# Attention scores of two heads as three products on half-height tiles, in place of two full-height products for each head

## Chip, cores and metric

The kernel runs on one core of a Trainium2 chip. The metric is device time in microseconds (us) of one execution. Engines are named as the profile names them: PE is TensorE's matmul, PEld its weight load, DVE is VectorE, ACT is ScalarE, POOL is GpSimd, SP is SyncE, which issues most DMAs.

## What is computed

One decoder layer on 512 tokens of width 1024, in float32: an RMSNorm, one input projection, two branches (an mLSTM with 4 heads of 128 and an attention with 8 heads of 64), gates, and an output projection added to the input. The change is in the attention scores. Blocks are 256 tokens long and the top 3 past blocks are taken, of which 512 tokens have at most one, so the attention is causal over all tokens. Cut to what matters:

```python
q = _rmsnorm(at_q.reshape(ha), q_norm_w)          # ha = (1, 512, 8, 64)
k = _rmsnorm(at_k.reshape(ha), k_norm_w)
...
s_own = jnp.einsum('bhqd,bhsd->bhqs', q_c, k_own) * scale - slopes[:, None, None] * dist_own
s_own = jnp.where(dist_own >= 0, s_own, -jnp.inf)
...
p = jax.nn.softmax(s_all, axis=-1)
```

`slopes` of head h is 2^-(h+1).

## The kernel before

[...] To keep float32 accuracy each operand is split into an upper part (the value cast to `float32r`, on ACT) and a lower part (the rest, a subtraction on DVE), and a product is a sum of upper x upper, upper x lower and lower x upper. The projections are done so, three products of 512 columns for each 128 rows of the contraction; they make up most of PE's work.

The attention works by pairs of heads, `g_pair(p)` for p = 0 to 3. PE transposes the pair's 128 columns of q and of k into a PSUM bank, 64 rows for either head. `g_q` and `g_k` then make three buffers for each head u: `qs[u]`, whose 64 own rows hold the upper part of q and whose other 64 rows hold the lower part; `kh[u]`, with the upper part of k in both halves; `kl[u]`, with the lower part of k in both halves. All these instructions work on 64 rows of 512 columns. With q's two parts stacked, a product over 128 rows with `kh` gives two of the terms at once, and one with `kl` the others. `g_attn(h, ...)` runs for one head: a POOL instruction scales the distances by the slope (`eh`), and for each of four row tiles `g_tile(i)` issues two products of 256, 256, 384 and 512 columns into one bank. DVE adds distances and finds the row's minimum, ACT exponentiates, DVE and POOL divide by the sum; `g_pt` transposes the result, and the second head's generator runs the products with v for both heads, as tiles of 128 rows by 64 columns, one for either head.

Nothing is issued when these functions call the engines. `Schedule` records each instruction with its estimated cost (`cost`, lines 219 to 248) and its dependencies, and `issue` sorts all engines' instructions by list scheduling; the order in which PE, DVE, ACT, POOL and SP then run is fixed. Any cost that changes can move instructions anywhere in the program. Nearly all instructions carry one line of the helper that issues them, L256.

Of the kernel before, what the change touches and what calls it, by code (L numbers as in the profile page):

```python
# [17 lines left out]
P = 128  # L18
# [171 lines left out]
class Schedule:  # L190
# [28 lines left out]
    def cost(self, eng, name, out, ins, args, kw):  # L219
        n = 1  # L220
        for d in (args[1] if name == "tensor_reduce" else out).shape[1:]:
            n *= d
        if name.startswith("dma"):
            return 1000.0 if eng == "gpsimd" else 100.0
        if eng == "tensor":
            if name == "transpose":
                return 109.0
            n = 1
            for d in kw["rhs"].shape[1:]:
                n *= d  # L230
            if kw["rhs"].dtype == F32R:
                return max(0.452 * n, 60.0) + 2.0
            return max(n, 64) * 4 * (0.43 if out.shape[0] == P else 0.21)
        if eng == "scalar":
            c = 180.0 + 0.85 * n
            if name == "activation":
                c += 95.0 * sum(isinstance(kw.get(k), bass.AP) for k in ("scale", "bias"))
            return c + (190.0 if "accum_out" in kw else 0.0)
        if eng == "gpsimd":
            return 330.0 + 190.0 * n if kw.get("op") == ALU.pow else 380.0 + 1.05 * n  # L240
        if name == "tensor_tensor_scan":
            return 1210.0
        if name == "tensor_copy" and not any(r[0].startswith("bank") for r in ins):
            return 160.0 + 0.52 * n
        c = 155.0 + 1.04 * n
        if name == "scalar_tensor_tensor" and len(ins) > 2:
            c += 60.0
        return c + (83.0 if "accum_out" in kw else 0.0)

    def add(self, eng, name, fn, args, kw):  # L250
# [125 lines left out]
def hybrid_layer(ctx: ExitStack, tc: tile.TileContext, xT, x, w_in, w_out, smalls, out):  # L376
# [40 lines left out]
    def transpose(out_, in_, idn):  # L417
        plan.now += 107.0
        nc.tensor.transpose(out_, in_, idn)
# [3 lines left out]
    def tiny(n):  # L423
        ntiny[0] += n
        return tinies[:, ntiny[0] - n:ntiny[0]]
# [152 lines left out]
    def need_w(name, kk):  # L578
        plan.until(lambda: (name, kk) in W)
        return W[name, kk]  # L580


    ident = sb("ident", [P, P])
    make_identity(tc.nc, ident)
# [222 lines left out]
    offs = [0, 128, 384, 768]  # L807

    def g_pair(p):
        rank = 5 + p / 100  # L810
        yield when(lambda: have["q"] == NT and have["k"] == NT and br.ok(6) and (p < 2 or 2 * p - 3 in pts))
        qs, kh, kl = ([br.get() for _ in range(2)] for _ in range(3))
        qw, kw = sm[:, C_QW:C_QW + 1], sm[:, C_KW:C_KW + 1]
        mine, other = (slice(0, 64), slice(64, 128)), (slice(64, 128), slice(0, 64))
        done = []

        def turn(src):
            ps = banks.get()
            for t in range(NT):
                transpose(ps[:, t * P:(t + 1) * P], src[:, t, p * P:(p + 1) * P], ident)  # L820
            have["A"] += 1
            return ps

        def g_q():
            yield pe_bank()
            ps = turn(tq)
            yield plan.now + SLACK
            for u in range(2):
                r = mine[u]
                t_ = act.activation(qs[u][r], ps[r], AF.Copy, scale=qw[r])  # L830
            yield t_
            for u in range(2):
                r = mine[u]
                t_ = dve.scalar_tensor_tensor(qs[u][other[u]], ps[r], qw[r], qs[u][r].bitcast(F32),
                                              op0=ALU.mult, op1=ALU.subtract)
            banks.put(t_, ps)
            done.append(t_)

        def g_k():
            yield pe_bank()  # L840
            ps = turn(tk)
            yield plan.now + SLACK
            for u in range(2):
                r = mine[u]
                t_ = act.activation(kh[u][r], ps[r], AF.Copy, scale=kw[r])
            yield t_
            for u in range(2):
                r = mine[u]
                act.activation(kh[u][other[u]], ps[r], AF.Copy, scale=kw[r])
                dve.scalar_tensor_tensor(kl[u][r], ps[r], kw[r], kh[u][r].bitcast(F32),  # L850
                                         op0=ALU.mult, op1=ALU.subtract)
                t_ = dve.tensor_copy(kl[u][other[u]], kl[u][r].bitcast(F32))
            t_ = max(t_, act.clock + SLACK)
            banks.put(t_, ps)
            done.append(t_)

        plan.add(g_q(), rank)
        plan.add(g_k(), rank)
        yield when(lambda: len(done) == 2)
        for u in range(2):  # L860
            plan.add(g_attn(2 * p + u, qs[u], kh[u], kl[u], max(done)), rank + u / 200)

    def g_attn(h, qs, kh, kl, t0):
        rank = 5 + h / 200
        yield when(lambda: b2.ok() and b5.ok() and (h < 2 or h - 2 in pts))
        eh, pr = b2.get(), b5.get()
        te = pool.tensor_scalar(eh, dist, 2.0 ** -(h + 1), 0.0, op0=ALU.mult, op1=ALU.add)
        mn, sums, rec = (tiny(NT) for _ in range(3))
        done = {"p": 0, "t": 0}
        at = [t0]  # L870

        def finish(key, t):
            at[0] = max(at[0], t)
            done[key] += 1

        def g_tile(i):
            n = P * (i + 1)
            nn = max(n, 256)
            yield pe_bank(max(at[0], te))
            ps = banks.get()  # L880
            ts = slice(i * P, (i + 1) * P)
            mm(ps[:, :nn], qs[:, ts], kh[:, :nn], True, False)
            mm(ps[:, :nn], qs[:, ts], kl[:, :nn], False, True)
            yield plan.now + SLACK
            p_ = pr[:, offs[i]:offs[i] + n]
            t_ = dve.tensor_tensor_reduce(p_, ps[:, :n], eh[:, S - n:], scale=-1.0, scalar=BIG,
                                          op0=ALU.add, op1=ALU.min, accum_out=mn[:, i:i + 1])
            banks.put(t_, ps)
            yield t_
            yield act.activation(p_, p_, AF.Exp, scale=-1.0, bias=mn[:, i:i + 1], accum_out=sums[:, i:i + 1])  # L890
            have["exp"] += 1
            dve.reciprocal(rec[:, i:i + 1], sums[:, i:i + 1])
            yield dve.clock + SLACK
            finish("p", pool.tensor_scalar(p_, p_, rec[:, i:i + 1], 1.0, op0=ALU.mult, op1=ALU.mult))

        def g_pt(a, blocks, pt):
            yield pe_bank(at[0])
            ps = banks.get()
            n = P * len(blocks)
            for b, (i, j) in enumerate(blocks):  # L900
                transpose(ps[:, b * P:(b + 1) * P], pr[:, offs[i] + j * P:offs[i] + (j + 1) * P], ident)
            yield plan.now + SLACK
            t_ = (act.copy, dve.tensor_copy, act.copy)[a](pt[:, 512 * a:512 * a + n], ps[:, :n])
            banks.put(t_, ps)
            finish("t", t_)

        for i in range(NT):
            plan.add(g_tile(i), rank)
        yield when(lambda: done["p"] == NT and b5.ok())
        b2.put(plan.now, eh)  # L910
        br.put(plan.now, qs, kh, kl)
        pt = b5.get()
        for a, blocks in enumerate(([(0, 0), (1, 0), (2, 0), (3, 0)],
                                    [(1, 1), (2, 1), (3, 1), (3, 3)],
                                    [(2, 2), (3, 2)])):
            plan.add(g_pt(a, blocks, pt), rank)
        yield when(lambda: done["t"] == 3)
        b5.put(plan.now, pr)
        pts[h] = (pt, [pt[:, 0:512], pt[:, 512:896], pt[:, 1024:1280], pt[:, 896:1024]], at[0])
        if h % 2 == 0:  # L920
            return
        yield when(lambda: h - 1 in pts and have["v"] == NT)
# [12 lines left out]
        have["at"] += 1  # L935
# [694 lines left out]
```

## Time and profile before

| | |
|---|---|
| median of 3 runs | 303.6 us (303.38 to 303.67) |
| profiled execution | 303.79 us |
| its span, first to last instruction | 302.1 us |
| granted TensorE clock, mean | 0.998 |
| busy, share of the span: PE, PEld, DVE, ACT, POOL | 98, 79, 75, 61, 27% |

The span leaves out 1.7 us around the instructions. [...] In the timeline, consecutive instructions with the same names are merged into a row with a count and the first one's shape. A `float32` product that is not a transpose leaves two records.

### The profile page before, as it was taken

The numbers are of one execution on the slowest core, as the hardware profiler recorded it, in microseconds if no ns is written. First come the engines' busy times: TensorE is split into PE (matmuls) and PEld (weight loads), VectorE is DVE, ScalarE is ACT, GpSimd is POOL, SyncE is SP. The second block draws the span as 40 slices with busy tenths as digits, with TensorE's granted clock in tenths as the row PEclk, the third lists the DMA queues.
The fourth block names the chain that finished last, engine by engine and source line by source line (L and its number), as shares of the span: only waits on it lengthen the run. The fifth ranks groups of instructions, "written<-read, shape, count | busy, mean of one in ns | idle before, by whom it ended". The sixth has DMA issues, their size and how long they took to land.

```text
span 302.1 us, 4336 instructions
## 1 busy us (share of the span) xinstructions
PE 296.0 (98%) x1534; PEld 239.5 (79%) x1534; DVE 226.0 (75%) x473; ACT 184.0 (61%) x327; POOL 82.5 (27%) x93
## 2 busy tenths in 40 slices
PE   8999999999999999999999999999999999999995
PEld 3999888888888888688678868578889987787784
DVE  4896979698788868968669988620348858799992
ACT  3594648874639718543767946993963526688500
POOL 3000201059440370127127017541001146131200
PEclk9999999999999999999999999999999999999999
DMA  6994793552224112203004040926007699964344
GB/s 202 397 415 189 190 285 104 106 172 94 84 72 150 60 69 72 69 0 106 37 1 141 0 139 2 301 47 138 3 1 219 158 288 245 203 142 69 47 148 154
DMA packets 13381, 40.19 MB, mean 133 GB/s; under 512 B 1584, under 2 KB 1840, under 8 KB 13360
## 3 DMA queue, kind: packets, MB, share of 16 engines
q1 hardware_dynamic: 10640, 32.05, 30.2%
q0 software_dynamic: 2720, 7.87, 15.2%
q8 instruction: 12, 0.20, 0.3%
q14 instruction: 9, 0.07, 0.1%
HBM read 37.81 MB, written 2.10 MB: 132 GB/s over the span
## 4 chain that ended last, share of the span: by engine, by line
PE 96%; DMA 1%; ACT 1%; DVE 1%; issue 1%; SPq 0%
PE bank L256 96%; DMA b<-in_w_in_dram 1%; DVE b L256 0%; ACT whi L256 0%; ACT br L256 0%; ACT xh L256 0%; DVE whi L256 0%; SPq L256 0%; SPq L369 0%
## 5 line engine op out<-in xcount | busy, mean ns | idle before, releaser
L256 PE MATMUL bank<-whi,xh 128*128 128x512 f32 (+2 forms) x220 | 70.8, 365 | 0.4 <-DVE whi L256 0.2
L256 PE MATMUL bank<-whi,xl 128*128 128x512 f32 (+2 forms) x220 | 70.5, 360 | 0.0
L256 PE MATMUL bank<-wlo,xh 128*128 128x512 f32 (+2 forms) x220 | 70.3, 359 | 0.0
L256 DVE TENSOR_TENSOR wlo<-raw,whi 128x1024 fp32r<-128x1024 f32 x35 | 43.6, 1248 | 3.2 <-ACT whi L256 2.9
L256 ACT CAST whi<-raw 128x1024 fp32r<-128x1024 f32 x35 | 36.7, 1047 | 14.2 <-PE bank L256 14.0
L256 PEld LDWEIGHTS bank<-whi,xh 128*128 128x128 f32 x220 | 38.5, 192 | 8.2 <-ACT xh L256 1.1
L256 PEld LDWEIGHTS bank<-whi,xl 128*128 128x128 f32 x220 | 37.9, 188 | 6.3 <-issue 0.2
L256 PEld LDWEIGHTS bank<-wlo,xh 128*128 128x128 f32 x220 | 37.9, 188 | 6.1
L256 POOL TENSOR_SCALAR b<-b,tinies 128x128 f32<-128x128 f32 (+3 forms) x32 | 31.8, 1007 | 39.0 <-DVE tinies L256 38.4
L256 PE MATMUL bank<-xh,whi 128*128 128x512 f32 x96 | 39.3, 410 | 0.0
L256 PE MATMUL bank<-xh,wlo 128*128 128x512 f32 x96 | 38.3, 400 | 0.0
L256 PE MATMUL bank<-xl,whi 128*128 128x512 f32 x96 | 38.1, 398 | 0.0
L256 PE MATMUL bank<-whi,br 128*128 128x512 f32 x112 | 36.1, 397 | 0.8 <-ACT br L256 0.8
L256 PEld LDWEIGHTS bank<-whi,br 128*128 128x128 f32 x112 | 21.0, 188 | 6.0 <-ACT br L256 1.2
L256 ACT ACTIVATE b<-b,tinies 128x128 f32<-128x128 f32 (+3 forms) x32 | 17.8, 556 | 12.9 <-DVE tinies L256 12.7
L256 PE MATMUL bank<-wlo,br 128*128 128x512 f32 x56 | 22.1, 397 | 0.0
L256 POOL TENSOR_TENSOR tinies<-tinies,mhalf 128x8 f32<-128x8 f32 (+1 forms) x12 | 19.8, 1660 | 7.8 <-DVE tinies L256 7.5
L256 PEld LDWEIGHTS bank<-xh,wlo 128*128 128x128 f32 x96 | 18.0, 188 | 4.4 <-issue 0.6
L256 PEld LDWEIGHTS bank<-xl,whi 128*128 128x128 f32 x96 | 18.1, 189 | 3.4 <-issue 0.4
L256 PEld LDWEIGHTS bank<-xh,whi 128*128 128x128 f32 x96 | 18.1, 189 | 3.4 <-issue 0.2
L256 DVE CUSTOM_DVE_ANT_0 b<-bank,b 128x128 f32<-128x128 f32 (+3 forms) x32 | 15.0, 488 | 4.8 <-PE bank L256 3.5
L256 PE MATMUL bank<-ident,b 128*128 128x128 f32 (+1 forms) x104 | 18.5, 268 | 0.0
(170 smaller groups left out, 490.7 us busy)
## 6 DMA issues: line engine op xcount, KB each, us to landing
raw<-in_w_in_dram SPq DMA_DIRECT2D x28, 512.0 KB, 3.6
raw<-in_w_out_dram SPq DMA_DIRECT2D x5, 512.0 KB, 4.4
vbuf<-in_x_dram SPq DMA_DIRECT2D x4, 512.0 KB, 7.5
out_dram<-b SPq DMA_DIRECT2D x7, 256.0 KB, 2.1
b<-in_w_in_dram SPq DMA_DIRECT2D x3, 520.0 KB, 7.5
raw<-in_w_out_dram POOLq DMA_DIRECT2D x3, 512.0 KB, 5.4
b<-in_x_dram POOLq DMA_DIRECT2D x6, 256.0 KB, 3.8
tq<-in_xT_dram SPq DMA_DIRECT2D x4, 256.0 KB, 5.2
```

The lines of the kernel that those rows point to most:

```text
L256: op = {"eng": eng, "fn": lambda: fn(*args, **kw), "cost": self.cost(eng, name, out, ins, args, kw), "n": len(self.ops), "table": next((se ...
```

## The change

One pair of heads is now one unit. `g_part` makes four buffers for the pair, `qh`, `ql`, `kh` and `kl`, each with 64 rows for either head: one ACT instruction on 128 rows for an upper part and one DVE instruction on 128 rows for a lower part. `g_attn` runs once for a pair. A row tile takes two banks at a time and issues six products over 64 rows each: for the terms qh x kh, qh x kl and ql x kh, in turn, the even head's on rows 0 to 63 into one bank and the odd head's on rows 64 to 127 into the other. The built program gives them a tile of 64 rows by 128 columns each, at row 0 or 64, which is also what it gives to four products of the mLSTM branch in both kernels (`mrow,sel`, over 36 rows).

Both heads share the distances scaled by the even head's slope. The odd head's slope is half of that, so its q is doubled, by a POOL instruction at the program's start that multiplies 64 values of the q norm's weights, and its scores are then multiplied by -0.5 instead of -1. Three numbers of the scheduler's cost function change too: a product over 64 rows is entered at half its cost, a POOL instruction at 120 ns more, a DVE instruction of a scalar and two tensors at 40 ns more.

```diff
             if kw["rhs"].dtype == F32R:
-                return max(0.452 * n, 60.0) + 2.0
+                return (max(0.452 * n, 60.0) + 2.0) * (0.5 if kw["rhs"].shape[0] == 64 else 1.0)
...
-            return 330.0 + 190.0 * n if kw.get("op") == ALU.pow else 380.0 + 1.05 * n
+            return 330.0 + 190.0 * n if kw.get("op") == ALU.pow else 500.0 + 1.05 * n
...
-            c += 60.0
+            c += 100.0
...
+    nc.gpsimd.tensor_scalar(sm[64:128, C_QW:C_QW + 1], sm[64:128, C_QW:C_QW + 1], 2.0, 0.0, op0=ALU.mult, op1=ALU.add)
     ident = sb("ident", [P, P])
...
-        qs, kh, kl = ([br.get() for _ in range(2)] for _ in range(3))
+        parts = [br.get() for _ in range(4)]
...
-            for u in range(2):
-                r = mine[u]
-                t_ = act.activation(qs[u][r], ps[r], AF.Copy, scale=qw[r])
-            yield t_
-            for u in range(2):
-                r = mine[u]
-                t_ = dve.scalar_tensor_tensor(qs[u][other[u]], ps[r], qw[r], qs[u][r].bitcast(F32),
-                                              op0=ALU.mult, op1=ALU.subtract)
...
-                act.activation(kh[u][other[u]], ps[r], AF.Copy, scale=kw[r])
...
-                t_ = dve.tensor_copy(kl[u][other[u]], kl[u][r].bitcast(F32))
...
+            yield act.activation(hi, ps, AF.Copy, scale=w)
+            t_ = dve.scalar_tensor_tensor(lo, ps, w, hi.bitcast(F32), op0=ALU.mult, op1=ALU.subtract)
...
-        te = pool.tensor_scalar(eh, dist, 2.0 ** -(h + 1), 0.0, op0=ALU.mult, op1=ALU.add)
+        te = pool.tensor_scalar(eh, dist, 2.0 ** -(2 * p + 1), 0.0, op0=ALU.mult, op1=ALU.add)
...
-            mm(ps[:, :nn], qs[:, ts], kh[:, :nn], True, False)
-            mm(ps[:, :nn], qs[:, ts], kl[:, :nn], False, True)
+            for a, b in ((qh, kh), (qh, kl), (ql, kh)):
+                for u in range(2):
+                    r = slice(64 * u, 64 * u + 64)
+                    mm(ps[u][:, :nn], a[r, ts], b[r, :nn], a is qh and b is kh, a is ql)
...
-            t_ = dve.tensor_tensor_reduce(p_, ps[:, :n], eh[:, S - n:], scale=-1.0, scalar=BIG,
+            t_ = dve.tensor_tensor_reduce(p_, ps[:, :n], eh[:, S - n:], scale=-0.5 if u else -1.0, scalar=BIG,
```

How the order on PE moves is shown at three places. In these rows the operand that is streamed stands first behind the arrow, then the weights; `br` are the buffers of the score operands, `xh`, `xl`, `whi` and `wlo` the parts of a projection's operands.

PE in the kernel before, the first pair's even head, right behind the rows of a projection. `br_0` is `qs`, `br_2` is `kh`, `br_4` is `kl`; each bank is one row tile:

```order
L256 MATMUL bank1_81<-br_2_74,br_0_72 128x256
L256 MATMUL bank1_81<-br_4_76,br_0_72 128x256
L256 MATMUL bank2_82<-br_2_74,br_0_72 128x256
L256 MATMUL bank2_82<-br_4_76,br_0_72 128x256
L256 MATMUL bank4_84<-br_2_74,br_0_72 128x384
L256 MATMUL bank4_84<-br_4_76,br_0_72 128x384
L256 MATMUL bank6_86<-br_2_74,br_0_72 128x512
L256 MATMUL bank6_86<-br_4_76,br_0_72 128x512
L256 MATMUL bank0_80<-xh_106,whi4_116 128x512
```

All eight products of a head stand together, between full-height products of the projection.

PE in the changed kernel, the first pair of heads. `br_0` is `qh`, `br_1` is `ql`, `br_2` is `kh`, `br_3` is `kl`; banks 4, 0 and 7 belong to the even head (rows 0 to 63), banks 6 and 3 to the odd one (rows 64 to 127):

```order
L257 MATMUL bank4_84<-br_2_74,br_0_72 128x256
L257 MATMUL bank6_86<-br_2_74,br_0_72 128x256
L257 MATMUL bank4_84<-br_3_75,br_0_72 128x256
L257 MATMUL bank6_86<-br_3_75,br_0_72 128x256
L257 MATMUL bank3_83<-br_2_74,br_0_72 128x256
L257 MATMUL bank3_83<-br_3_75,br_0_72 128x256
L257 MATMUL bank2_82<-xl_107,whi5_118 128x512
L257 MATMUL bank4_84<-br_2_74,br_1_73 128x256
L257 MATMUL bank2_82<-xh_106,wlo5_119 128x512
L257 MATMUL bank2_82<-xh_106,whi0_108 128x512
L257 MATMUL bank7_87<-br_2_74,br_0_72 128x384
L257 MATMUL bank7_87<-br_3_75,br_0_72 128x384
```

The scheduler sorts the six products of a tile singly, so that full-height products of the projection now stand among them.

PE in the changed kernel, the third row tile of the second pair. `br_4` is `qh`, `br_5` is `ql`, `br_6` is `kh`, `br_7` is `kl`; bank 1 is the even head's, bank 4 the odd head's:

```order
L257 MATMUL bank1_81<-br_6_78,br_4_76 128x384
L257 MATMUL bank1_81<-br_7_79,br_4_76 128x384
L257 MATMUL bank1_81<-br_6_78,br_5_77 128x384
L257 MATMUL bank3_83<-xh_106,whi5_118 128x512
L257 MATMUL bank3_83<-xl_107,whi5_118 128x512
L257 MATMUL bank4_84<-br_6_78,br_4_76 128x384
L257 MATMUL bank4_84<-br_7_79,br_4_76 128x384
L257 MATMUL bank4_84<-br_6_78,br_5_77 128x384
```

Here the even head's three products stand alone, then two full-height products, then the odd head's three.

## Rows read from the trace of the kernel before

**Rows 1.** The page: busy time of each engine; the chain that ended last, by engine.

```profile
PE 296.0 (98%) x1534; PEld 239.5 (79%) x1534; DVE 226.0 (75%) x473; ACT 184.0 (61%) x327; POOL 82.5 (27%) x93
PE 96%; DMA 1%; ACT 1%; DVE 1%; issue 1%; SPq 0%
```

**Rows 2.** Waits of PE: who waited for whom, total us, times, longest us.

```profile
PE bank L369 <- DVE warm L369: 1.2, 1, 1.2
PE bank L256 <- ACT br L256: 0.8, 1, 0.8
PE bank L256 <- DVE whi L256: 0.2, 1, 0.2
PE bank L256 <- DVE b L256: 0.2, 1, 0.2
```

**Rows 3.** Timeline of PE (start us, duration us, what, count): one head's eight products.

```profile
98.06 1.45 PE L256 MATMUL bank<-br,br 128*128 128x256 f32 x8
99.34 0.40 PE L256 MATMUL bank<-xh,whi 128*128 128x512 f32 x1
```

**Rows 4.** Groups by shape (busy us, mean ns, idle before): operands of the scores.

```profile
L256 ACT ACTIVATE br<-bank,sm 64x512 fp32r<-64x512 f32 x24 | 16.3, 683 | 2.3 <-PE bank L256 1.3 <-ACT br L256 0.5
...
L256 DVE SCALAR_TENSOR_TENSOR br<-bank,sm,br 64x512 fp32r<-64x512 f32 x16 | 12.0, 750 | 3.5 <-ACT br L256 3.0
...
L256 DVE CAST br<-br 64x512 fp32r<-64x512 f32 x8 | 3.4, 420 | 0.2
L256 DVE SCALAR_TENSOR_TENSOR xl<-tq,sm,xh 128x512 fp32r<-128x512 f32 x4 | 2.9, 744 | 0.0
```

**Rows 5.** Timeline of PE, 190.7 to 193.3 us: transposes, half-height products, transposes.

```profile
190.72 0.71 PE L256 MATMUL bank<-ident,b 128*128 128x128 f32 x5
191.36 0.49 PE L256 MATMUL bank<-mrow,sel 36*128 36x512 f32 x1
191.78 0.55 PE L256 MATMUL bank<-ident,b 128*128 128x128 f32 x3
192.26 0.73 PE L256 MATMUL bank<-mrow,sel 36*128 36x512 f32 x2
192.92 0.44 PE L256 MATMUL bank<-ident,b 128*128 128x128 f32 x2
193.28 1.07 PE L256 MATMUL bank<-b,vbuf 128*64 128x512 f32 x2
```

**Rows 6.** Timeline of PE, 120.3 to 123.6 us: a projection, half-width tiles, the projection.

```profile
120.32 0.39 PE L256 MATMUL bank<-xh,wlo 128*128 128x512 f32 x1
120.55 0.39 PE L256 MATMUL bank<-xh,whi 128*128 128x512 f32 x1
120.87 2.16 PE L256 MATMUL bank<-b,vbuf 128*64 128x512 f32 x12
122.95 0.50 PE L256 MATMUL bank<-xl,whi 128*128 128x512 f32 x1
123.29 0.40 PE L256 MATMUL bank<-xh,wlo 128*128 128x512 f32 x1
```

**Rows 7.** Products of v's tile on PE, stretches 198.2:199.1 and 198.2:199.5: durations ns, starts, forms.

```profile
L256 PE MATMUL bank<-b,vbuf x5: 379/537/643, 198.3 to 199.0; 128*64 128x512 f32 x2, 128*64 128x384 f32 x2, 128*64 128x256 f32 x1
...
L256 PE MATMUL bank<-b,vbuf x8: 272/486/643, 198.3 to 199.4; 128*64 128x384 f32 x3, 128*64 128x512 f32 x2, 128*64 128x256 f32 x2, 128*64 128x128 f32 x1
```

**Rows 8.** The start: timeline of POOL and DVE; DMA issues (KB, us to landing).

```profile
0.79 0.39 SPq L369 DMA_DIRECT2D sm<-in_smalls_dram  x1
...
1.07 0.29 POOL masks.py:199 TENSOR_SCALAR_AFFINE_SELECT ident<-ident 128x128 f32<-128x128 f32 x1
...
1.40 0.89 DVE L369 TENSOR_TENSOR sel<-ident 36x128 fp32r<-36x128 f32 x4 [0.20 <-POOL ident masks.py:199]
...
5.33 0.43 DVE L256 CAST whi<-b 128x520 fp32r<-128x520 f32 x1 [3.05 <-DMA b<-in_w_in_dram]
...
sm<-in_smalls_dram SPq DMA_DIRECT2D x1, 31.0 KB, 1.9
```

More of the change, by code (lines that the diff above doesn't have):

```diff
@@ L810, in g_pair, with g_part @@
         rank = 5 + p / 100
-        yield when(lambda: have["q"] == NT and have["k"] == NT and br.ok(6) and (p < 2 or 2 * p - 3 in pts))
-        qs, kh, kl = ([br.get() for _ in range(2)] for _ in range(3))
-        qw, kw = sm[:, C_QW:C_QW + 1], sm[:, C_KW:C_KW + 1]
-        mine, other = (slice(0, 64), slice(64, 128)), (slice(64, 128), slice(0, 64))
+        yield when(lambda: have["q"] == NT and have["k"] == NT and br.ok(4) and (p < 2 or 2 * p - 3 in pts))
+        parts = [br.get() for _ in range(4)]
         done = []
-        def turn(src):
+        def g_part(src, hi, lo, w):
+            yield pe_bank()
             ps = banks.get()
@@ L821, in turn @@
             have["A"] += 1
[L822 to L826, printed above, removed]
             yield plan.now + SLACK
-            for u in range(2):
-                r = mine[u]
-                t_ = act.activation(qs[u][r], ps[r], AF.Copy, scale=qw[r])
-            yield t_
-            for u in range(2):
-                r = mine[u]
-                t_ = dve.scalar_tensor_tensor(qs[u][other[u]], ps[r], qw[r], qs[u][r].bitcast(F32),
-                                              op0=ALU.mult, op1=ALU.subtract)
+            yield act.activation(hi, ps, AF.Copy, scale=w)
@@ L836, in g_q @@
+            t_ = dve.scalar_tensor_tensor(lo, ps, w, hi.bitcast(F32), op0=ALU.mult, op1=ALU.subtract)
             banks.put(t_, ps)
             done.append(t_)
[L839 to L848, printed above, removed]
-                act.activation(kh[u][other[u]], ps[r], AF.Copy, scale=kw[r])
-                dve.scalar_tensor_tensor(kl[u][r], ps[r], kw[r], kh[u][r].bitcast(F32),
-                                         op0=ALU.mult, op1=ALU.subtract)
-                t_ = dve.tensor_copy(kl[u][other[u]], kl[u][r].bitcast(F32))
-            t_ = max(t_, act.clock + SLACK)
-            banks.put(t_, ps)
-            done.append(t_)
@@ L857, in g_pair @@
-        plan.add(g_q(), rank)
-        plan.add(g_k(), rank)
-        yield when(lambda: len(done) == 2)
[L860 to L866, printed above, removed]
-        te = pool.tensor_scalar(eh, dist, 2.0 ** -(h + 1), 0.0, op0=ALU.mult, op1=ALU.add)
[L868 to L874, printed above, removed]
+        plan.add(g_part(tq, *parts[0:2], sm[:, C_QW:C_QW + 1]), rank)
@@ new lines, in g_pair, with g_attn, finish @@
+        plan.add(g_part(tk, *parts[2:4], sm[:, C_KW:C_KW + 1]), rank)
+        yield when(lambda: len(done) == 2)
+        plan.add(g_attn(p, *parts, max(done)), rank)
+    def g_attn(p, qh, ql, kh, kl, t0):
+        rank = 5 + p / 100
+        yield when(lambda: b2.ok() and b5.ok(2) and (p < 2 or 2 * p - 3 in pts))
+        eh, prs = b2.get(), [b5.get() for _ in range(2)]
+        te = pool.tensor_scalar(eh, dist, 2.0 ** -(2 * p + 1), 0.0, op0=ALU.mult, op1=ALU.add)
+        mn, sums, rec = ([tiny(NT) for _ in range(2)] for _ in range(3))
+        done = {"p": [0, 0], "t": [0, 0]}
+        at = [t0, t0]
+        def finish(key, u, t):
+            at[u] = max(at[u], t)
+            done[key][u] += 1
@@ L878, in g_tile, with g_soft, g_pt @@
             nn = max(n, 256)
-            yield pe_bank(max(at[0], te))
-            ps = banks.get()
+            yield (max(*at, te), lambda: banks.ok(KEEP + 1), True)
+            ps = [banks.get() for _ in range(2)]
             ts = slice(i * P, (i + 1) * P)
-            mm(ps[:, :nn], qs[:, ts], kh[:, :nn], True, False)
-            mm(ps[:, :nn], qs[:, ts], kl[:, :nn], False, True)
-            yield plan.now + SLACK
-            p_ = pr[:, offs[i]:offs[i] + n]
-            t_ = dve.tensor_tensor_reduce(p_, ps[:, :n], eh[:, S - n:], scale=-1.0, scalar=BIG,
-                                          op0=ALU.add, op1=ALU.min, accum_out=mn[:, i:i + 1])
+            now = plan.now
+            for a, b in ((qh, kh), (qh, kl), (ql, kh)):
+                for u in range(2):
+                    r = slice(64 * u, 64 * u + 64)
+                    mm(ps[u][:, :nn], a[r, ts], b[r, :nn], a is qh and b is kh, a is ql)
+            plan.now = (now + plan.now) / 2
+            for u in range(2):
+                plan.add(g_soft(u, i, n, ps[u]), rank, plan.now + SLACK)
+        def g_soft(u, i, n, ps):
+            p_ = prs[u][:, offs[i]:offs[i] + n]
+            t_ = dve.tensor_tensor_reduce(p_, ps[:, :n], eh[:, S - n:], scale=-0.5 if u else -1.0, scalar=BIG,
+                                          op0=ALU.add, op1=ALU.min, accum_out=mn[u][:, i:i + 1])
             banks.put(t_, ps)
             yield t_
-            yield act.activation(p_, p_, AF.Exp, scale=-1.0, bias=mn[:, i:i + 1], accum_out=sums[:, i:i + 1])
+            yield act.activation(p_, p_, AF.Exp, scale=-1.0, bias=mn[u][:, i:i + 1], accum_out=sums[u][:, i:i + 1])
             have["exp"] += 1
-            dve.reciprocal(rec[:, i:i + 1], sums[:, i:i + 1])
+            dve.reciprocal(rec[u][:, i:i + 1], sums[u][:, i:i + 1])
             yield dve.clock + SLACK
-            finish("p", pool.tensor_scalar(p_, p_, rec[:, i:i + 1], 1.0, op0=ALU.mult, op1=ALU.mult))
-        def g_pt(a, blocks, pt):
-            yield pe_bank(at[0])
+            finish("p", u, pool.tensor_scalar(p_, p_, rec[u][:, i:i + 1], 1.0, op0=ALU.mult, op1=ALU.mult))
+        def g_pt(u, a, blocks, pt):
+            yield pe_bank(at[u])
             ps = banks.get()
@@ L900, in g_pt @@
             for b, (i, j) in enumerate(blocks):
-                transpose(ps[:, b * P:(b + 1) * P], pr[:, offs[i] + j * P:offs[i] + (j + 1) * P], ident)
+                transpose(ps[:, b * P:(b + 1) * P], prs[u][:, offs[i] + j * P:offs[i] + (j + 1) * P], ident)
             yield plan.now + SLACK
@@ L904, in g_pt, with g_turn @@
             banks.put(t_, ps)
-            finish("t", t_)
+            finish("t", u, t_)
+        def g_turn(u):
+            yield when(lambda: done["p"][u] == NT and b5.ok())
+            pt = b5.get()
+            for a, blocks in enumerate(([(0, 0), (1, 0), (2, 0), (3, 0)],
+                                        [(1, 1), (2, 1), (3, 1), (3, 3)],
+                                        [(2, 2), (3, 2)])):
+                plan.add(g_pt(u, a, blocks, pt), rank)
+            yield when(lambda: done["t"][u] == 3)
+            b5.put(plan.now, prs[u])
+            pts[2 * p + u] = (pt, [pt[:, 0:512], pt[:, 512:896], pt[:, 1024:1280], pt[:, 896:1024]], at[u])
         for i in range(NT):
             plan.add(g_tile(i), rank)
-        yield when(lambda: done["p"] == NT and b5.ok())
+        for u in range(2):
+            plan.add(g_turn(u), rank + u / 200)
+        yield when(lambda: sum(done["p"]) == 2 * NT)
         b2.put(plan.now, eh)
[L911 to L922, printed above, removed]
+        br.put(plan.now, qh, ql, kh, kl)
+        h = 2 * p + 1
+        yield when(lambda: h in pts and h - 1 in pts and have["v"] == NT)
         yield pe_bank(max(pts[h][2], pts[h - 1][2]))
```

## The prediction

> **What bounds the kernel now.** I read the page first, then the waits, then the timeline of PE. The page shows PE busy for 98% of the span and holding 96% of the chain that ended last [rows 1]. Busy time alone would not show that PE is the limit, since its records overlap; the waits do. PE waits four times in the whole span, 2.4 us in total, of which 1.2 and 0.2 us stand at the very start; only 0.8 and 0.2 us fall later [rows 2]. So PE's queue is the path. What makes PE's queue longer or shorter moves the end by as much, and what ACT, DVE or POOL save can give back 1.0 us at most.
>
> The second thing to read is the distance from one matmul's start to the next. One head's eight products run from 98.06 to 99.34, when the projection goes on: 1.28 us for 2816 streamed columns (2 x (256 + 256 + 384 + 512)), or 0.4545 ns a column [rows 3]. A projection product of 512 columns takes 0.23 us, 120.32 to 120.55 [rows 6], the same rate. The eight heads' scores therefore cost 8 x 1.28 = 10.24 us of PE. That is all there is to save on the path.
>
> **The streamed columns.** Before, 64 products stream 22,528 columns. After, 96 products stream 33,792. One behind the other they take 33,792 x 0.4545 = 15.36 us, 5.12 us more than before. Two products on different halves of the array can run side by side, and if all did, 7.68 us would be left. But only products that stand together can. I counted in the order of the changed kernel: the 96 products form 22 stretches with full-height or half-width work between them. Thirteen stretches hold one head alone (36 products, 12,544 columns: six of 3 x 384, four of 3 x 256, and 768, 1536 and 256 columns). Nine hold both heads: four of six products of 256 and one of six of 512 that alternate between the heads; one of 256 that alternates and ends with three of the odd head; two with three of 512 of the even head and then three of the odd head; one of twelve products, grouped by head. With a stretch as long as its longer head, these nine stream 1024 + 3072 + 1536 + 3072 + 2688 = 11,392 columns. So the floor is 23,936 columns, 10.88 us, which is 0.64 us more than before, and the ceiling is 15.36 us.
>
> No row shows two half-height tiles at once. The nearest is the products with v, on two tiles of 128 rows by 64 columns. Two records belong to a product there; one product of 512 columns alone fills a row of 1.07 us, while twelve records, two heads' products of 512, 384 and 256 columns, are through in 2.08 us, 120.87 to 122.95 [rows 5, 6]. These tiles run side by side, and one even runs ahead: in the stretch from 198.3 the program's sequence is 512, 384, 384, 256, 256, 128 columns with the heads in turn, and by 199.4 a record of 128 has started while only three of the four records of 384 and two of the four of 256 have [rows 7]. The sixth product has passed the fifth. I take full overlap for the alternating stretches and half of the overlap for the three grouped ones, where a product would have to pass two or three of the other head's (the pair of two 512 stretches then costs 2 x 768 columns more, the one of twelve 832): 26,304 columns, 11.96 us, **1.7 us more** than before, with +0.64 and +5.12 as ends.
>
> [...]
>
> **The changes of tile shape.** Before, the scores have the shape of the projections around them and pay nothing for standing among them. After, every stretch is a change of shape and back. The price stands in the trace. Coming from a projection to another shape, the last full product takes 0.32 us to the next start (120.55 to 120.87) in place of 0.23: +0.09 [rows 6]. Inside, half-height products with 64 by 128 tiles take 0.42 us for one of 512 columns (191.36 to 191.78) and 0.66 us for two (192.26 to 192.92), in place of 0.23 and 0.46: +0.19 and +0.20 once for a stretch, whatever its length [rows 5]. [...] Back in the projection, the first product takes 0.34 us (122.95 to 123.29): +0.11 [rows 6]. A round trip is 0.09 + 0.20 + 0.11 = 0.40 us. It costs more than a whole product of 512 columns. Two of the 22 stretches touch work that already had another shape, which saves 0.2 us each. 22 x 0.40 - 2 x 0.20 = **8.4 us more**. The least that I can defend is the 0.20 us that the half-height rows show by themselves, 4.4 us; a change of shape cannot gain time, since it streams nothing.
>
> **Off the path.** ACT drops from 24 to 8 instructions at 683 ns: -10.9 us. DVE drops 16 of 750 ns and 8 of 420 ns, 15.4 us, and gains 8 on 128 rows, for which the row with the same shape has 744 ns: 6.0 us, so -9.4 us [rows 4]. Four scalings of the distances leave POOL. Nothing on PE waits for these beyond the 1.0 us above, so I count zero. The transposes of q, k and of the softmax, the evacuations, the exponentials and the DMAs keep their number. The new costs in the scheduler move instructions on every engine; PE gets 10 us longer while the others get shorter, so they should run earlier against it. I allow 1.0 us of gain and 2 us of loss, less than two waits like PE's longest [rows 2].
>
> The multiplication by 2 stands on POOL ahead of the identity, and waits for the small parameters: issued at 0.79 us, landed 1.9 us later, 2.7 us [rows 8]. Behind it in POOL's queue are the identity (0.3 us) and, waiting for that on DVE, the four instructions that make `sel` (0.89 us); they would end near 4.4 us. DVE's first work for PE waits for a DMA until 5.33 us, so 0.9 us of cover is left [rows 8]. I count zero; without that cover a late `sel` would push the first cast and the end one for one.
>
> **The sum**, against the profiled execution's 303.79 us: + 1.7 + 8.4 = 313.9 us. The median lies 0.2 us under that execution, so **313.7 us**.
>
> **Rivals.** (1) The tiles do not run side by side, or their weight loads follow each other so that the short products gain nothing: 15.36 us of streaming, 303.6 + 5.1 + 8.4 = 317.1 us. Against it speak rows 6 and 7, for it that those are tiles of another shape. (2) The new order puts a wait on PE, at a bank or at an operand, of the size of its longest one now, once or twice: 315 to 316.5 us. For it speaks that two banks are taken at a time; against it, that a slower PE gives everyone more time. (3) Cheaper changes: only the 0.20 us inside a stretch is paid, since a projection product may hide the rest: 303.6 + 1.7 + 4.4 = 309.7 us. Rows 6 speak against it at both ends of a stretch. With changes that cost nothing and the floor in streaming it would be 304.2 us, less up to 1.0 us of waits: no change. (4) The other side: the 96 products all run two at a time, also where the even head's three and the odd head's three are parted by a projection product, and changes are free: 303.6 - 2.56 = 301.0 us. It decides if a round trip costs under 0.09 us (2.0 us over 22 stretches); rows 5 show twice that for half of the trip, and a full-height product between two stretches uses all rows.
>
> [...]
>
> **Chances.** Forecast, 312 to 315: 0.62. Rival 1: 0.13. Rival 2: 0.08. Rival 3: 0.12 for 309.7 and what lies between it and 312; 0.03 for no change. Rival 4: 0.02. The range 310.5 to 317.5 leaves out the cheap half of rival 3, rival 4 and the worst sums of rivals 1 and 2, together not quite 0.2. A measurement of this kernel tells about 0.2% (0.6 us) from no change: faster 0.02, within 0.03, slower 0.95.
>
> **What the profile after would show.** PE still without waits and with about 10 us more from the first score to the last product with v; rows like "128 rows by 128" to "64 by 128" with 0.32 us in place of 0.23 at each of 22 stretches; in alternating stretches, starts of the two heads within some ns and six products of 256 in about 0.36 us plus 0.20; in grouped ones a start of the odd head during the even head's products. Wrong would be: pairs of starts 0.12 us apart (rival 1), a wait above 1 us on PE in the attention (rival 2), or 0.23 us across a change of shape (rivals 3, 4).

## The result, and the profile after

| | before | after |
|---|---|---|
| median | 303.49 us (303.31 to 303.67, 4 runs) | 311.28 us (310.9 to 311.59, 4 runs) |
| profiled execution | 303.79 us | 310.9 us |
| its span | 302.1 us | 309.2 us |

After / before is 1.026, with a 95% interval of 1.024 to 1.027: 7.8 us slower, where +10.1 us had been forecast. The mean granted clock is 1.000. The page of after, busy time and the chain that ended last, answers to [rows 1]:

```profile
PE 304.3 (98%) x1566; PEld 238.2 (77%) x1566; DVE 215.5 (70%) x457; ACT 169.7 (55%) x309; POOL 68.8 (22%) x90
...
PE 98%; DVE 0%; issue 0%
```

DVE lost 10.5 us of work, ACT 14.3 and POOL 13.7, and PE is still the whole path. Waits of PE (who waited for whom, total us, times, longest), which answer to [rows 2]; the 0.8 and the two of 0.2 us are gone:

```profile
PE bank L370 <- DVE warm L370: 1.2, 1, 1.2
```

The timeline of PE and its weight loads (PEld) around one stretch of six score products, three of either head, 256 columns each (start us, duration us, instruction, count, idle before):

```profile
102.95 0.39 PE L257 MATMUL bank<-xh,wlo 128*128 128x512 f32 x1
103.27 0.41 PEld L257 LDWEIGHTS bank<-br,br 64*128 64x128 f32 x6 [0.36 <-issue]
103.27 0.62 PE L257 MATMUL bank<-br,br 64*128 64x256 f32 x6
...
103.82 0.19 PEld L257 LDWEIGHTS bank<-xh,whi 128*128 128x128 f32 x1
103.82 0.50 PE L257 MATMUL bank<-xh,whi 128*128 128x512 f32 x1
103.92 0.19 PEld L257 LDWEIGHTS bank<-xl,whi 128*128 128x128 f32 x1
104.15 0.40 PE L257 MATMUL bank<-xl,whi 128*128 128x512 f32 x1
```

Read the starts, not the durations: a projection product is recorded with 0.39 us, and the next one starts 0.23 us after it. 102.95 to 103.27 is 0.32 us in place of 0.23 for the last projection product: +0.09. The stretch holds PE from 103.27 to 103.82, 0.55 us; 768 columns at 0.4545 ns are 0.35 us: +0.20, and two heads in the time of one. 103.82 to 104.15 is 0.33 in place of 0.23: +0.10. A round trip is 0.39 us. PEld differs at both ends: inside the projection the next weights are loaded ahead (103.92 for 104.15), but those of the new shape start at 103.27, with the matmul, after 0.36 us in which PEld waited for nothing that the profile shows, and those of the way back at 103.82, again with theirs. Such "issue" waits of PEld ahead of a bank, in total, times and longest, in after:

```profile
PEld bank L257 <- issue: 16.5, 52, 0.8
```

and in before:

```profile
PEld bank L256 <- issue: 9.6, 31, 0.8
```

That is 21 more, for 22 new stretches. The two heads of the stretch at 103.27 start within 6 ns: a window to 103.269 us holds one product, one to 103.275 us both (durations, first and last start, shapes):

```profile
L257 PE MATMUL bank<-br,br x1: 383/383/383, 103.3 to 103.3; 64*128 64x256 f32 x1
...
L257 PE MATMUL bank<-br,br x2: 382/382/383, 103.3 to 103.3; 64*128 64x256 f32 x2
```

Here the heads alternate. In the stretch at 109.83 the even head's three products of 512 stand ahead of the odd head's three, and they start together too; the windows end at 109.836 and 109.845 us:

```profile
L257 PE MATMUL bank<-br,br x1: 493/493/493, 109.8 to 109.8; 64*128 64x512 f32 x1
...
L257 PE MATMUL bank<-br,br x2: 493/493/493, 109.8 to 109.8; 64*128 64x512 f32 x2
```

A stretch with one head alone pays the same trip for half of the use. Timeline of PE, three products of 256 of the even head:

```profile
150.40 0.39 PE L257 MATMUL bank<-xh,wlo 128*128 128x512 f32 x1
150.72 0.61 PE L257 MATMUL bank<-br,br 64*128 64x256 f32 x3
151.26 0.51 PE L257 MATMUL bank<-xh,whi 128*128 128x512 f32 x1
151.60 0.40 PE L257 MATMUL bank<-xl,whi 128*128 128x512 f32 x1
```

150.40 to 151.60 less two usual distances of 0.23 is 0.74 us, the same as for the six at 103.27. Measured so (last start ahead of a stretch to the second start behind it, less two usual distances), the 22 stretches take 19.70 us of PE, against 10.26 for before's 64 products: +9.4 us. Elsewhere PE saves: 0.4 us in the other odd shapes, and 1.9 us of stalls (3.14 to 1.27 us over the program, everything that is neither a usual distance nor one of these stretches; where two odd stretches touch, how the 2.3 us divides between these two sums is a choice). The sum, -2.3 + 9.4 = +7.1 us, is the difference of the two profiled executions. The rest to the medians' 7.8 us is that the profiled execution of after was the fastest of its four (310.9 against 311.28), and that of before lies 0.3 us over its median.

### The profile page after: what moved, and what is told of

The parts are those of the page before. It is cut to its first block, busy times and chain, and to the rows that moved or that the text cites. A ratio compares the mean times of both kernels' runs of the same rounds, so it can differ in the third digit from the quotient of the medians.

```text
span 309.2 us, 4351 instructions
## 1 busy us (share of the span) xinstructions
PE 304.3 (98%) x1566; PEld 238.2 (77%) x1566; DVE 215.5 (70%) x457; ACT 169.7 (55%) x309; POOL 68.8 (22%) x90
## 4 chain that ended last, share of the span: by engine, by line
PE 98%; DVE 0%; issue 0%
PE bank L257 97%; PE bank L370 1%; DVE b L257 0%; DVE rstdb L370 0%; DVE warm L370 0%
## 5 line engine op out<-in xcount | busy, mean ns | idle before, releaser
L257 DVE TENSOR_TENSOR wlo<-raw,whi 128x1024 fp32r<-128x1024 f32 x35 | 42.5, 1220 | 21.8 <-ACT whi L257 21.7
L257 PE MATMUL bank<-xh,whi 128*128 128x512 f32 x96 | 41.1, 428 | 0.0
L257 PE MATMUL bank<-xh,wlo 128*128 128x512 f32 x96 | 39.4, 411 | 0.0
L257 PE MATMUL bank<-xl,whi 128*128 128x512 f32 x96 | 39.3, 409 | 0.0
L257 POOL TENSOR_SCALAR b<-b,tinies 128x128 f32<-128x128 f32 (+3 forms) x32 | 23.1, 732 | 44.1 <-DVE tinies L257 40.3
L257 POOL TENSOR_TENSOR tinies<-tinies,mhalf 128x8 f32<-128x8 f32 (+1 forms) x12 | 18.3, 1546 | 7.0 <-DVE tinies L257 6.8
```

The lines of the kernel that those rows point to most:

```text
L257: op = {"eng": eng, "fn": lambda: fn(*args, **kw), "cost": self.cost(eng, name, out, ins, args, kw), "n": len(self.ops), "table": next((se ...
```

## The experiments

Each kernel is compared with the kernel before on the same chip, whose medians there were 303.45 to 303.57 us. "PE's time for the scores" is measured as above.

**Six products in one piece.** In the changed kernel the six products of a row tile are recorded as one operation (with the sum of their costs), so that the scheduler can't part them. 15 stretches are left.

```diff
+            nc.together, nc.unit = True, None
             for a, b in ((qh, kh), (qh, kl), (ql, kh)):
...
+            nc.together, nc.unit = False, None
```

> The six products of a row tile are recorded as one unit, so that the scheduler can't put anything among them: 15 stretches of half-height products instead of 22, all of them with both heads. Theory A (a change of shape costs 0.20 us each way, a stretch lasts as long as its longer head): 29 changes of shape more than the kernel before instead of 42 (-2.6 us) and 7.7 us of streaming instead of 10.9 (-3.2 us) against the changed kernel's 311.3, so 305.5 us, still 2 us slower than before. Theory B (the new order of everything else and its waits make the loss): no more than 1 us from 311.3. Theory C (the tiles don't run side by side): only the 2.6 us, 308.7.

Measured: 305.45 us (305.25 to 305.66), 1.005 of before (1.003 to 1.007). PE's time for the scores is 13.48 us; less 7.68 us of streaming that is 5.80 us for 15 trips, 0.387 us each.

**Four stretches.** Besides, row tiles 0 and 1 share a bank, and all 24 products of a pair are one operation.

```diff
-        def g_tile(i):
+        def g_tile(rows):
...
-        for i in range(NT):
-            plan.add(g_tile(i), rank)
+        for rows in (((0, 1), 2, 3),):
+            plan.add(g_tile(rows), rank)
```

> All 24 products of a pair of heads as one unit: row tiles 0 and 1 share a bank for each head, so that a pair needs six banks, and the half-height products stand in 4 stretches. Theory A: 12 changes of shape more than the kernel before instead of 42 (-6.0 us) and 7.7 us of streaming instead of 10.9 (-3.2 us), so 302.1 us, 1.4 us faster than before. Theory B (order and waits): six banks at a time make PE or the evacuations wait more, 305 us or more.

Measured: 301.4 us (301.25 to 301.59), 0.992 of before (0.989 to 0.995). So the same arithmetic, with its products left together, is faster than before. Timeline of PE, one pair's scores:

```profile
97.28 0.40 PE L258 MATMUL bank<-xh,whi 128*128 128x512 f32 x1
97.60 2.21 PE L258 MATMUL bank<-br,br 64*128 64x256 f32 x24
99.74 0.50 PE L258 MATMUL bank<-xl,whi 128*128 128x512 f32 x1
100.08 0.39 PE L258 MATMUL bank<-xh,wlo 128*128 128x512 f32 x1
```

97.28 to 100.08 less 0.46 is 2.34 us, of which 4224 columns are 1.92: 0.42 us for the trip. The four take 9.34 us, less than before's 10.26.

**Eight stretches.** The same with 18 and 6 products; how many free banks a group waits for follows its size.

```diff
-        for rows in (((0, 1), 2, 3),):
+        for rows in (((0, 1), 2), (3,)):
```

> Each pair's 24 products in two stretches (18 and 6 products), so 8 stretches in place of 4 in the run with four, and 16 changes of shape over the kernel before in place of 12. Streaming side by side stays 7.68 us. Theory (0.40 us for a round trip): against the run with four stretches, 4 more changes of 0.20 us, 301.4 + 0.8 = 302.2 us. Rival (the four-stretch run is fast through its order elsewhere, not through its few changes of shape): no difference, 301.4 us, within 0.3.

Measured: 303.03 us (302.84 to 303.37), 0.999 of before (0.998 to 1.000). It is 1.6 us slower than with four, so the rival falls, and the theory's 0.8 was too little: I had counted the changes of the whole program, in which the new order has one stretch of products with v and one of `mrow,sel` fewer, and priced them all alike. The scores alone show the price: 10.85 us against 9.34, 0.38 us for each of four trips. What the fewer other stretches should have given back, 0.8 us, came to 0.1 us.

| kernel | stretches of scores | streaming us | PE's time for the scores us | for one trip us |
|---|---|---|---|---|
| four stretches | 4 | 7.68 | 9.34 | 0.42 |
| eight stretches | 8 | 7.68 | 10.85 | 0.40 |
| six in one piece | 15 | 7.68 | 13.48 | 0.39 |
| changed kernel | 22 | 10.88 | 19.70 | 0.40 |

**Grouped by head.** "Six in one piece", with the even head's three products ahead of the odd head's three.

```diff
-            for a, b in ((qh, kh), (qh, kl), (ql, kh)):
-                for u in range(2):
+            for u in range(2):
+                for a, b in ((qh, kh), (qh, kl), (ql, kh)):
```

> The run with joined stretches, with the six products of a row tile in another order: the even head's three first, then the odd head's three, in place of the heads in turn. Number and place of the stretches (15), of the changes of shape and of the streamed columns stay. Theory (a product on the other half of the array starts as soon as its own half is free, also past three earlier products of the other head): 305.4 us, no difference from the joined run, and starts of the two heads some ns apart. Half overlap, as the prediction counted grouped stretches: of the 7.68 us that side by side saves, half is lost, up to 309.3 us. Matmuls strictly in the program's order: up to 313.1 us.

Measured: 305.64 us (305.53 to 305.73), 1.007 of before (1.006 to 1.009); 13.58 us for the scores against 13.48. The two kernels have the same order on every engine but for these six products, so in groups of three their order is worth 0.1 us of PE's time. Half overlap (309.3 us) and products strictly in the program's order (313.1 us) are 3.7 and 7.5 us away.

**Twelve by head.** How far can a product pass? The 24 products of a stretch (in the version with joined products with v, below), twelve of the even head ahead of twelve of the odd one.

```diff
+            for u in range(2):
+                for pair, ps in got:
...
                         for a, b in ((qh, kh), (qh, kl), (ql, kh)):
-                            for u in range(2):
```

> The run with four stretches and joined products with v, with the 24 products of a stretch grouped by head: the even head's twelve (4224 columns, 1.92 us), then the odd head's twelve. No more changes of shape. Two mechanisms: the odd head's half of the array is free, so its products start at once however many of the even head's stand ahead: 298.7 us, starts of the two heads some ns apart. Or a product can pass about three others, as in the grouped run, and no more: the odd head starts when three of the even head's twelve are left, 2688 columns or 1.22 us late in each of four stretches, 298.7 + 4.9 = 303.6 us. With no passing at all 298.7 + 7.7 = 306.4 us.

Measured: 303.43 us (303.26 to 303.77), 4.7 us over the version with the heads in turn (298.69 us), as the mechanism with three passed products gives (4.9 us). Products of PE from 97.5 to 98.84 us, and to 98.9 us:

```profile
L258 PE MATMUL bank<-br,br x8: 275/278/381, 97.7 to 98.7; 64*128 64x256 f32 x6, 64*128 64x384 f32 x2
...
L258 PE MATMUL bank<-br,br x10: 275/306/383, 97.7 to 98.9; 64*128 64x256 f32 x7, 64*128 64x384 f32 x3
```

The even head has six products of 256, three of 384 and three of 512, in this order. Up to 98.84 its first eight have started and nothing else. Then its third of 384, the ninth, starts, and with it a seventh product of 256, which is the odd head's first: it passes the three of 512 and had waited as long as there were more. Each of the four stretches takes 3.50 us in place of 2.33.

The changed kernel's own trace agrees, in another arrangement. In its stretch of twelve products at 98.49 the issued order is one of the odd head, three of the even, one odd, then the even head's 384 and three of 512, then the odd head's three of 384. The odd head's two products of 256 have started by 98.72, so its half is free from about 98.84 (256 columns are 0.12 us), but its first of 384 starts only when the even head's 384 has, with three of 512 left to pass. Windows to 98.959 and to 98.965 us:

```profile
L257 PE MATMUL bank<-br,br x6: 275/305/381, 98.5 to 99.0; 64*128 64x256 f32 x5, 64*128 64x384 f32 x1
...
L257 PE MATMUL bank<-br,br x7: 275/333/437, 98.5 to 99.0; 64*128 64x256 f32 x5, 64*128 64x384 f32 x2
```

**Full height.** The changed kernel's order on every engine, but its 96 score products over all 128 rows, both heads' at once. Their cost in the scheduler stays at half, so that the order stays too. Nothing changes shape and nothing runs side by side.

```diff
-                    mm(ps[u][:, :nn], a[r, ts], b[r, :nn], a is qh and b is kh, a is ql)
+                    mm(ps[u][:, :nn], a[:, ts], b[:, :nn], a is qh and b is kh, a is ql)
```

> The changed kernel in the very same order on every engine, with each of the 96 products over all 128 rows instead of 64. The scores of both heads are thus added up, so this part of the result is another. No change of shape is left, and no two products can run side by side. Theory A: the scores on PE cost 33,792 columns, 15.4 us, instead of the 19.7 us that the changed kernel's trace gives for its 22 stretches: 311.3 - 4.3 = 307.0 us. Theory B (order and waits): 311 us or more. If changes of shape cost nothing and pairing is all: 311.3 + 4.5 = 315.8 us.

Measured: 307.55 us (307.37 to 307.58), 1.012 of before (1.009 to 1.015). Timeline of PE, the six products that answer to those at 103.27 above:

```profile
102.39 0.39 PE L257 MATMUL bank<-xh,wlo 128*128 128x512 f32 x1
102.62 0.87 PE L257 MATMUL bank<-br,br 128*128 128x256 f32 x6
103.32 0.40 PE L257 MATMUL bank<-xh,whi 128*128 128x512 f32 x1
103.56 0.40 PE L257 MATMUL bank<-xl,whi 128*128 128x512 f32 x1
```

102.62 to 103.32 is 0.70 us, 1536 columns one behind the other, and the distances ahead and behind are 0.23 and 0.24. So six half-height products side by side (0.74 us with their trip) gain nothing over six at full height, and three alone lose 0.39 us. In this order half height costs 311.28 - 307.55 = 3.7 us. The time is close to the 307.0 us of theory A. PE waits as in after: behind the start not at all, and at the start 1.0 us for DVE's first cast, which in after had come earlier.

**The costs alone.** The kernel before with the changed costs of POOL and DVE.

```diff
-            return 330.0 + 190.0 * n if kw.get("op") == ALU.pow else 380.0 + 1.05 * n
+            return 330.0 + 190.0 * n if kw.get("op") == ALU.pow else 500.0 + 1.05 * n
...
-            c += 60.0
+            c += 100.0
```

> The kernel before with the two changed costs of POOL and DVE in the scheduler's function and nothing else of the change. Theory A: these move the order but no work, PE has 1.0 us of waits to lose after its start: 302.5 to 304.5 us. Theory B (the order makes the loss): well above 305.

Measured: 304.3 us (304.21 to 304.51), 1.002 of before (1.001 to 1.004). Waits of PE:

```profile
PE bank L256 <- DVE whi L256: 1.1, 1, 1.1
PE bank L256 <- DVE b L256: 1.1, 2, 0.9
PE bank L256 <- DVE br L256: 0.3, 1, 0.3
```

The 1.1 us for `whi` stands at the start; the others, 1.4 us, come later, where before has 1.0. The new order alone moves the time by 0.7 us, here upwards.

**Products with v in one piece.** The kernel before, with a pair's eight products with v recorded as one operation; nothing else. Four stretches in place of nine.

```diff
+        nc.together, nc.unit = True, None
         for j in range(NT):
             for g in (h - 1, h):
...
-            if j < NT - 1:
-                yield pe()
+        nc.together, nc.unit = False, None
```

> The kernel before with its full-height scores; each pair's eight products with v joined into one stretch, nothing else. 12 changes of shape fewer than before (14 against 26). Theory (0.20 us for a change): 303.6 - 2.4 = 301.2 us. Rival (a change costs nothing for half-width tiles): 303.6 us; if PE has to wait for the last transposed tile of the softmax: above 303.6 us.

Measured: 299.34 us (299.22 to 299.67), 0.987 of before (0.985 to 0.988): 4.2 us faster, where 2.4 had been expected. What was missed is in the timeline of PE of the kernel before: one head's product of 512 (two records) alone between two transposes.

```profile
148.13 0.27 PE L256 MATMUL bank<-ident,b 128*128 128x128 f32 x1
148.33 1.07 PE L256 MATMUL bank<-b,vbuf 128*64 128x512 f32 x2
149.33 0.33 PE L256 MATMUL bank<-ident,b 128*128 128x128 f32 x1
```

This version has all sixteen records in one stretch:

```profile
120.53 0.40 PE L257 MATMUL bank<-xh,wlo 128*128 128x512 f32 x1
120.86 2.37 PE L257 MATMUL bank<-b,vbuf 128*64 128x512 f32 x16
123.16 0.50 PE L257 MATMUL bank<-xh,whi 128*128 128x512 f32 x1
123.50 0.40 PE L257 MATMUL bank<-xl,whi 128*128 128x512 f32 x1
```

120.53 to 123.50 less 0.46 is 2.51 us; four such are 10.03 us, where the nine stretches took 13.35. Of the 3.3 us, five trips of 0.40 are 2.0. I put the other 1.3 us down to overlap that was lost where the heads stood apart; it is what remains, and was not measured by itself. The new order also saves 0.7 us in `mrow,sel` and 0.6 us of stalls, together 4.6 us between the profiled executions.

**Both.** Four stretches of scores, and the edit just shown: four of products with v.

> The run with four stretches, and besides each pair's eight products with v joined into one stretch, so that 16 changes of shape fewer are left than in it (22 in the whole program, against 26 in the kernel before). Theory (0.40 us for a round trip, whatever the tile): 301.4 - 3.2 = 298.2 us. Rival (half-width tiles pay less for a change, or joining them makes PE wait for the softmax): 299.5 to 301.5 us.

Measured: 298.69 us (298.65 to 298.8), 0.984 of before (0.983 to 0.986). Against four stretches alone PE saves 3.3 us in the products with v and 0.4 in `mrow,sel`, and stalls 1.0 us longer. The half-height scores themselves give only 299.34 - 298.69 = 0.65 us over full-height ones, no more than a new order alone moved the time above.

**Operands on 64 rows.** This version, with the eight ACT and eight DVE instructions of the score operands split in two halves of 64 rows again.

```diff
-            yield act.activation(hi, ps, AF.Copy, scale=w)
-            t_ = dve.scalar_tensor_tensor(lo, ps, w, hi.bitcast(F32), op0=ALU.mult, op1=ALU.subtract)
+            for r in (slice(0, 64), slice(64, 128)):
+                t_ = act.activation(hi[r], ps[r], AF.Copy, scale=w[r])
+            yield t_
+            for r in (slice(0, 64), slice(64, 128)):
+                t_ = dve.scalar_tensor_tensor(lo[r], ps[r], w[r], hi[r].bitcast(F32), op0=ALU.mult, op1=ALU.subtract)
```

> The run with four stretches and joined products with v, with the operands of the scores made on 64 rows again: each of the eight ACT and eight DVE instructions on 128 rows becomes two on 64 rows, so ACT gets 8 x 683 ns = 5.5 us and DVE 8 x 750 ns = 6.0 us longer. The scheduler's new order gives the products of mrow and sel four stretches in place of two, 2 x 0.40 = 0.8 us. Theory (ACT and DVE are off the path): 298.7 + 0.8 = 299.5 us. Rival (the time that the change took from ACT and DVE is what took PE's waits away): these come back at a bank or an operand, 300.5 us or more, and stand among the waits of PE.

Measured: 298.2 us (298.13 to 298.25), 0.982 of before (0.979 to 0.984), the fastest of all. Its page and the waits of PE:

```profile
PE 290.8 (98%) x1566; PEld 235.4 (79%) x1566; DVE 220.4 (74%) x465; ACT 175.1 (59%) x318; POOL 71.7 (24%) x90
...
PE bank L379 <- DVE warm L379: 1.2, 1, 1.2
PE bank L258 <- DVE whi L258: 0.9, 1, 0.9
```

ACT and DVE are 5.6 and 6.2 us busier than in the version without the split, PE has no wait behind the start, and the time is 0.5 us shorter, not longer. The 0.8 us for `mrow,sel` came as 0.75, but the stalls fell by 1.2 us, which neither side had expected; 0.5 us of it is a wait at 271.25 us that the version without the split has. So the rival falls for these 5.6 and 6.2 us: in this order they are worth nothing on the path. Against before ACT and DVE are still 8.9 and 5.6 us less busy, and that part was not given back.

## Why the prediction was right, and where it was off

The forecast was 313.7 us; the median of 311.28 lies in the range, 2.4 us lower. The mechanism was the forecast one: the trips between shapes cost more than side-by-side products give. The number was less good than it looks. It lies below the 312 to 315 us that had 0.62, in the band given to rival 3 with 0.12, and not by rival 3's cheaper trips: the overlap was 1.1 us better than counted, and 1.9 us of stalls went that the sum did not have.

- **What bounds it: right.** PE's queue is the path before and after, and the 5.6 and 6.2 us added to ACT and DVE in the last experiment cost nothing.
- **Streamed columns: floor right, picked value too high.** The step that failed is "half of the overlap for the three grouped ones": 11.96 us in place of 10.88, 1.08 us too much. In groups of three nothing is lost, as the stretch at 109.83 (0.90 us to 110.73, of which 1536 columns are 0.70 and 0.20 stand inside) and the grouped run (13.58 us against 13.48) show. The stretch of twelve is not two groups, as I had counted it, but changes heads four times; it holds PE from 98.49 to 99.92, 1.43 us, and less the 0.20 inside that is the 1.22 us of its longer head's 2688 columns. So all three overlap in full. It is a mis-sized term; a loss came with groups of twelve, 1.17 us a stretch.
- **Changes of shape: right.** 8.4 us predicted; 19.70 - 10.88 = 8.8 us measured. The three parts (0.09, 0.20, 0.11) stand in the timeline at 102.95 to 104.15 as 0.09, 0.20 and 0.10, although the prices came from other tiles. That the trip is paid once for a stretch, whatever its length, holds from 3 to 24 products (0.39 to 0.42 us).
- **Waits: counted at zero, 1.9 us were gained.** I had allowed 1.0 us of gain, the two later waits of [rows 2], and these went. They did not stand among the scores, whose last product starts at 184.0 us: the 0.2 us stood at 195.58, and the 0.8 us in the output projection:

```profile
279.61 0.50 PE L256 MATMUL bank<-whi,br 128*128 128x512 f32 x1 [0.78 <-ACT br L256]
```

  Some 0.45 us more are the start of the profiled execution, where DVE's first cast began at 4.88 us in place of 5.33 because its weights had landed earlier. That differs between executions: full height has after's order on every engine, and there the cast began at 5.45. The rest, 0.4 us, is scattered. A slower PE does not explain the two waits: with four stretches PE spends less on the scores than in before (9.34 us against 10.26) and has no wait behind the start either. The free time of ACT and DVE was tested in part (operands on 64 rows), and no wait came back. Waits behind the start go with the order: the three pairs of kernels that share it (after and full height, six in one piece and grouped by head, both and twelve by head) agree, with none, none and one of 0.5 us. Why an order is good stays open.
- **Off the path: right in effect.** The score operands of after, to be read beside [rows 4]:

```profile
L257 DVE SCALAR_TENSOR_TENSOR br<-bank,sm,br 128x512 fp32r<-128x512 f32 x8 | 5.7, 744 | 0.3 <-ACT br L257 0.2
L257 ACT ACTIVATE br<-bank,sm 128x512 fp32r<-128x512 f32 x8 | 5.3, 688 | 3.4 <-PE bank L257 3.4
```

  688 ns on 128 rows against 683 on 64, and 744 against 750: half of the rows were no cheaper. ACT and DVE lose 11.0 and 9.7 us here (16.3 - 5.3 and 15.4 - 5.7), where 10.9 and 9.4 had been worked out.
- **The multiplication at the start: right, with less cover than counted.** Timeline of POOL and DVE, beside [rows 8]:

```profile
2.78 0.19 POOL L370 TENSOR_SCALAR sm<-sm 64x1 f32<-64x1 f32 x1 [2.29 <-DMA sm<-in_smalls_dram]
...
3.31 0.29 POOL masks.py:199 TENSOR_SCALAR_AFFINE_SELECT ident<-ident 128x128 f32<-128x128 f32 x1
3.63 0.89 DVE L370 TENSOR_TENSOR sel<-ident 36x128 fp32r<-36x128 f32 x4 [2.44 <-POOL ident masks.py:199]
4.88 0.43 DVE L257 CAST whi<-b 128x520 fp32r<-128x520 f32 x1 [0.35 <-DMA b<-in_w_in_dram]
```

  `sel` ends at 4.52 us (4.4 had been worked out), and DVE then still waits 0.35 us for the weights, not 0.9, since these came earlier this time.
- **Rivals.** (1) fell: the two heads start 3 to 10 ns apart. (2) fell: no wait behind the start. (3) fell: the whole trip is paid, 0.09 and 0.10 us at the ends beside the 0.20 inside. (4) fell for this order; its gain needs few trips rather than cheap ones, and with four the kernel is faster than before.

The sum as it came, by the traces: scores +9.4 (forecast +10.1), other shapes -0.4, stalls -1.9, together +7.1 us between the profiled executions.

## What to carry to other kernels

Half-height products pay by the stretch: work out the columns saved and set the price of a trip, here 0.40 us, against every place where the shape changes and changes back, and count these places in the order that is really issued, not in the source. A scheduler that sorts products one by one, with no price for a change of shape, will tear such groups apart; recording them as one operation, 24 at a time, turned +2.6% into -0.8%, and the same for products with v, which nobody had set out to change, was worth more (-1.3%). Look for small tiles that stand alone: they pay the trip and lose their partner (three products of one head alone held PE for 0.74 us, as long as six of both).

## What the runs showed of the hardware that was not expected

- A product for a free half of the array passed up to three earlier products that had not started, and waited while there were more: full overlap in groups of three (two to pass), 1.17 us lost in each stretch with groups of twelve. Behind "three" stand the four stretches with groups of twelve, all with the same pattern, and the changed kernel's stretch at 98.49. Each product has its weight load; whether products or instructions are counted is not shown, and groups of other sizes were not tried.
- The trip had one price, 0.39 to 0.42 us, for 64 by 128 tiles with one half in use or both, and for 3 to 24 products. At 103.27 and 103.82 us the weights were not loaded ahead across a change, and PEld's "issue" waits ahead of a bank went from 31 to 52; that this makes the price is my reading, and whether a trip could be had without it was not tried.
